# Projecting the gates' 48 columns with the linear attention's values, token groups of 304 and 256 columns

## The chip, the cores and the metric

One NeuronCore of a Trainium2 chip runs the whole kernel. The metric is the device time of one execution in microseconds (us). A profiled execution also has a span, from its first to its last instruction.

Engines are named as in the profile: PE is the matrix engine, PEld its weight loads, DVE, ACT and POOL the vector, scalar and GpSimd engines, and SP the engine that issues nearly all DMAs here, one after the other, in the order of its queue. Each engine works through its own queue in order.

## What is computed

Two layers of a diffusion backbone over 256 context tokens and 2048 latent tokens, 1024 wide. In each layer the modulated stream is multiplied by one combined input projection whose columns feed three branches: gated DeltaNet (a), neighbourhood attention (b) and gated linear attention (c, "GLA"). The branches are gated, concatenated, projected and normalised.

```python
(a_qkv_l, a_ab_l, a_z_l, b_q_l, b_k_l, b_v_l, b_z_l,
 c_q_l, c_k_l, c_v_l, c_r_l, c_z_l) = jnp.split(ml @ w_in[i], PROJ_SPLITS, axis=-1)
...
oa_c, oa_l = gdn_branch(a_qkv_c, a_ab_c, a_qkv_l, a_ab_l, conv_w[i], a_log[i], dt_bias[i])
ob_c, ob_l = na_branch(b_q_c, b_k_c, b_v_c, b_q_l, b_k_l, b_v_l, rpb[i], ctx_out)
oc_c, oc_l = gla_branch(c_q_c, c_k_c, c_v_c, c_r_c, c_q_l, c_k_l, c_v_l, c_r_l,
                        gla_w2[i], gla_b2[i])
```

The 48 columns of this document are `c_r` (32, from which GLA's decay gates come) and `a_ab` (16, from which the DeltaNet's gates come).

## The kernel before

The 2304 tokens are cut into six blocks of 384, each of three tiles of 128 tokens. The modulated stream of a block lies in DRAM (`M`), 1024 rows deep, as eight k-tiles. `Dense.run` multiplies it by a set of weight columns. Each float32 product is made of three fp32r products (high by high, high by low, low by high), so one output group is 8 k-tiles by 3, or 24 matmuls, all from the one line L197 in `dense_mm`. There are two kinds of groups:

- a channel group (`chan`) has the weights as the stationary operand and 384 tokens moving; its output is columns by tokens;
- a token group (`tok`) has one tile's 128 tokens as the stationary operand and up to 512 weight columns moving; its output is tokens by columns.

In each layer the runs come in this order, and in each run the blocks one after another, first the channel groups of a block and then the token groups of its three tiles:

1. the GLA run: channel groups of 48 (`O_CR` and `O_AB`), 128 (`O_CK`) and 128 (`O_CQ`) columns; token groups of 512 (`O_CV` and `O_CZ`). It also splits the stream into high and low parts (L186, L189) and writes them back to DRAM (`MS`). `gla.block` (lines from L405 on) follows each block in program order;
2. the attention run: four channel groups of 128 columns and token groups of 512 (`O_BV` and `O_BZ`);
3. runs for the DeltaNet's convolution (channel groups only) and, later, its output gate (`O_AZ`, token groups of 512).

In layer 1 the two context tiles have no output gates, so their token groups in the first two runs are 256 wide.

A k-tile sits in an SBUF buffer called `mm`; there are ten buffers (`MBUF`), eight for the block at work and two for the next one. A buffer of the old block comes free when the block's last token group has read it, and only then does SP load the next block's k-tile into it (L241 from `MS`, L244 from `M`). Outputs of groups go through PSUM tiles of a pool with two buffers (`psd`).

The callback of the 48-column group, `cb_r`, copies its output (L367), writes the 32 `c_r` rows to DRAM as `RC` (L368), and turns the `a_ab` part by three transposes on PE (L371) into `e.ab`. `gla.block` reads `RC` back as `rc` and makes the gates from it (matmuls `pg`, L425), after the rotation matmuls `pr` (L417). Then follow a chain on DVE and ACT (L427 to L465), products on POOL (`qkp`, L472), small matmuls (`pD` L476, `pA` and `pB` L494 and L501, 32 or 64 columns wide), and per 128 tokens the matmuls `pO`, `pk`, `pS` with their copies. `gla.reverse` (L552 on) ends the branch.

The program's order is made by a scheduler at build time: it places the instructions on the engines by program order, by readiness and by a priority that callbacks and splits are given. Matmuls of the two runs therefore stand between those of `gla.block`, and the attention run begins while `gla.block` is still at work.

## Time and profile before

| what | us |
|---|---|
| median of three runs | 3960.82 |
| the three runs | 3960.82, 3921.74, 3962.12 |
| the profiled execution | 3949.59 |
| its span | 3947.8 |
| PE busy in the span | 3618.4 (92%) |
| DVE busy | 2455.6 (62%) |
| ACT busy | 1687.4 (43%) |

Busy time counts a matmul from its start to its modelled end; matmuls that follow each other overlap, so the pace of a stream is read from the distance of the starts. The granted clock is given as a share of the full TensorE clock (1.00 is 2.4 GHz, 0.5 is 1.2 GHz; a stretch between them holds some of each). "x<-y" in a row names what is written and what is read; a bracket gives the idle time ahead of a row and who ended it.

### The profile page before, as it was taken

What the parts mean: (1) busy time and instruction counts of PE and PEld (TensorE: products, weight loads), DVE (VectorE), ACT (ScalarE), POOL (GpSimd) and SP (SyncE); (2) the same over time, 40 slices, a digit from 0 to 9 for tenths busy, and PEclk for the clock granted to TensorE, in tenths of its full rate; (3) what the DMA queues carried; (4) which work ended last, traced back from release to release, by engine and by line L of the source; (5) the groups of instructions that cost most, each with busy time, mean ns of one, the idle gap of its engine ahead of it and who ended that gap; (6) DMA issues with size and microseconds to landing.
All of it is one profiled execution on the core that took longest, in us unless ns stands there. A gap on an engine that the chain in (4) does not pass through costs nothing.

```text
span 3947.8 us, 76664 instructions
## 1 busy us (share of the span) xinstructions
PE 3618.4 (92%) x27262; PEld 3113.5 (79%) x27262; DVE 2455.6 (62%) x6983; ACT 1687.4 (43%) x4587; POOL 682.8 (17%) x1118
## 2 busy tenths in 40 slices
PE   6999999999989999998998999999999899989898
PEld 3787778769977888896776778777899688878787
DVE  4456463668966477446884655427788567653577
ACT  3533233435533455565544333333455235545531
POOL 0221111220102222220002211102102132222100
PEclk8988889999999799999997889899999888879899
DMA  9844325886687777766755444468665977685664
GB/s 294 284 133 141 124 84 167 264 264 198 208 271 227 223 210 208 211 204 213 238 178 172 141 129 137 131 202 246 202 213 193 324 207 213 194 215 171 218 204 125
DMA packets 756085, 787.55 MB, mean 199 GB/s; under 512 B 190206, under 2 KB 665206, under 8 KB 755702
## 3 DMA queue, kind: packets, MB, share of 16 engines
q1 hardware_dynamic: 755702, 782.64, 64.5%
q8 instruction: 216, 3.54, 0.4%
q14 instruction: 167, 1.37, 0.1%
HBM read 548.41 MB, written 234.03 MB: 198 GB/s over the span
## 4 chain that ended last, share of the span: by engine, by line
PE 60%; DMA 18%; DVE 13%; ACT 4%; SPq 2%; issue 2%; POOL 1%; DVEq 0%; ACTq 0%; POOLq 0%
PE p L197 29%; PE py L197 6%; DMA mm<-MS 3%; PE p L1258 3%; DMA gb<-GR 2%; DMA o<-OA 1%; PE pv L1022 1%; PE po L1042 1%; PE pd L1029 1%; DMA kk<-KK 1%; PE p L104 1%; PE pk L1011 1%; PE po L1044 1%; DVE acc L661 1%; PE pD L476 1%
## 5 line engine op out<-in xcount | busy, mean ns | idle before, releaser
L197 PE MATMUL p<-mm,wh 128*128 128x384 f32 (+1 forms) x3648 | 995.8, 352 | 51.9 <-DMA mm<-MS 32.4
L197 PEld LDWEIGHTS p<-mm,wh 128*128 128x128 f32 (+1 forms) x3648 | 661.3, 191 | 123.2 <-DMA mm<-MS 48.1
L197 PE MATMUL p<-mm,wl 128*128 128x384 f32 (+1 forms) x1824 | 630.0, 347 | 0.4 <-DVE wl L189 0.3
L197 PE MATMUL p<-wh,mm 128*128 128x512 f32 (+1 forms) x1696 | 566.5, 407 | 11.4 <-DMA mm<-MS 4.5
L197 PEld LDWEIGHTS p<-wh,mm 128*128 128x128 f32 x1696 | 329.4, 197 | 89.7 <-DMA mm<-MS 9.2
L661 DVE SCALAR_TENSOR_TENSOR acc<-pre,cw,acc 128x384 f32<-128x384 f32 (+1 forms) x576 | 358.3, 640 | 49.8 <-ACT acc L659 43.0
L197 PEld LDWEIGHTS p<-mm,wl 128*128 128x128 f32 (+1 forms) x1824 | 346.5, 190 | 16.1 <-issue 9.7
L197 PE MATMUL p<-wl,mm 128*128 128x512 f32 (+1 forms) x848 | 342.4, 404 | 1.2 <-DVE rst L395 1.0
L197 PEld LDWEIGHTS p<-wl,mm 128*128 128x128 f32 x848 | 167.3, 197 | 36.2 <-issue 2.2
L197 PE MATMUL py<-w,mh 128*128 128x512 f32 x544 | 178.8, 407 | 7.7 <-ACT mh L1380 5.0
L1004 POOL TENSOR_TENSOR kd<-kk,eD 128x256 f32<-128x256 f32 x144 | 89.3, 620 | 453.2 <-DMA kk<-KK 190.0
L1274 DVE SCALAR_TENSOR_TENSOR zt<-zt,p 128x256 f32<-128x256 f32 (+1 forms) x102 | 51.5, 507 | 178.9 <-ACT zt L1273 177.9
L1237 ACT ACTIVATE w<-w,mn 128x696 f32<-128x696 f32 (+2 forms) x136 | 112.8, 830 | 82.8 <-DVE mn L1234 80.0
L651 POOL COPY pre<-pre 128x4 f32<-128x4 f32 x120 | 81.0, 678 | 383.8 <-DVE acc L661 190.9
L925 DVE TENSOR_TENSOR tmp<-M 96x30 f32<-96x30 f32 (+4 forms) x360 | 126.6, 352 | 29.7 <-issue 21.9
L1015 DVE SCALAR_TENSOR_TENSOR R<-pk,neG,kk 128x128 f32<-128x128 f32 x272 | 81.4, 344 | 100.9 <-PE pk L1011 100.0
L865 DVE SCALAR_TENSOR_TENSOR gb<-gb,Gt,mats 128x128 f32<-128x128 f32 x288 | 86.4, 359 | 91.4 <-DMA gb<-GR 88.9
L1258 PE MATMUL p<-v,wl 120*128 120x64 f32 (+1 forms) x960 | 140.5, 285 | 0.0
L926 DVE TENSOR_TENSOR M<-M,tmp 96x30 f32<-96x30 f32 (+4 forms) x360 | 127.3, 354 | 6.3
L1258 PEld LDWEIGHTS p<-v,wl 120*128 120x128 f32 (+1 forms) x960 | 130.6, 204 | 0.7
L186 ACT CAST wh<-raw 128x512 fp32r<-128x512 f32 (+3 forms) x144 | 75.8, 555 | 123.6 <-DMA raw<-in_w_in 105.7
L189 POOL TENSOR_TENSOR mm<-mm 128x384 fp32r<-128x384 f32 x48 | 58.4, 1222 | 398.2 <-ACT mm L186 391.7
(307 smaller groups left out, 8136.1 us busy)
## 6 DMA issues: line engine op xcount, KB each, us to landing
mm<-MS SPq DMA_DIRECT2D x384, 384.0 KB
kk<-KK SPq DMA_DIRECT2D x144, 512.0 KB
MS<-mm SPq DMA_DIRECT2D x96, 384.0 KB
raw<-in_w_in SPq DMA_DIRECT2D x104, 256.0 KB
w<-in_w_mod SPq DMA_DIRECT2D x96, 256.0 KB
M<-m SPq DMA_DIRECT2D x36, 512.0 KB
mm<-M SPq DMA_DIRECT2D x96, 192.0 KB
KK<-kq SPq DMA_DIRECT2D x96, 192.0 KB
```

Source lines behind the costliest of these rows:

```text
L186: eng_hi.copy(hi, src)
L189: eng_lo.tensor_tensor(lo, src, hi.bitcast(F32), op=ALU.subtract)
L197: e.nc.tensor.matmul(p, x(k), y(k), start=n == 0, stop=n == 3 * KD - 1)
L651: nc.gpsimd.tensor_copy(pre[:, 0:4], pre[:, m:m + 4])
L661: nc.vector.scalar_tensor_tensor(acc[:, :n], pre[:, k:k + n], w(kind, k), acc[:, :n], op0=ALU.mult, op1=ALU.add)
L865: nc.vector.scalar_tensor_tensor(E[:, d, h], gb[:, d, h], self.G[:, d, c, h0 + h:h0 + h + 1], e.mats[:, 1 + d], op0=ALU.subtract, op1=ALU.min)
L925: nc.vector.tensor_tensor(tv, col, row, op=ALU.mult)
L926: nc.vector.tensor_tensor(o, o, tv, op=ALU.add)
L1004: nc.gpsimd.tensor_tensor(kd, kv[:, :, 0], self.eD[:, d, c, h0:h0 + 2].unsqueeze(2).to_broadcast([128, 2, 128]), op=ALU.mult)
L1015: nc.vector.scalar_tensor_tensor(R[:, h], pk[:, h], sc(self.neG, h), kv[:, h, 1], op0=ALU.mult, op1=ALU.add)
L1237: nc.scalar.activation(w[:, a, 0:256 + nk], w[:, a, 0:256 + nk], AF.Exp, bias=m[:, a:a + 1], scale=-1.0, accum_out=sm[:, a:a + 1])
L1258: nc.tensor.matmul(p[:, a], l, r, start=j == 0, stop=j == len(parts) - 1)
```

## The change

The 48-column channel group is gone. Its columns join the values' token group: `O_CV` (256) with `O_CR` (32), which lie side by side in the weights, and `O_AB` (16), 304 moving columns. The output gate's 256 columns (`O_CZ`) form a second token group. The attention run's 512 are cut into 256 (`O_BV`) and 256 (`O_BZ`) too, so that the weight tiles of both runs have like sizes. The new callback `cb_v` copies 304 columns, writes the values, copies 16 columns into `e.ab`, and turns the 32 `c_r` columns by one transpose per tile into a PSUM tile that fills up over the block's three tiles; the block's `RC` is written after the third. The separate weight pool `w0` falls away.

```diff
-    def cb_r(self, P, ps):
-        def f(p, b):
-            e, nc = self.e, self.e.nc
-            r = P.tile([48, BLK], F32, tag="r48", name="r48", bufs=1)
-            nc.scalar.copy(r, p)
-            nc.sync.dma_start(self.RC[b], r[0:32])
-            pt = ps.tile([128, TPB, 48], F32, tag="dn", name="pt")
-            for t in range(TPB):
-                nc.tensor.transpose(pt[:, t], r[:, t * 128:(t + 1) * 128], e.ident[0:48, 0:48])
-            nc.vector.tensor_copy(e.ab[:, b * TPB:(b + 1) * TPB], pt[:, :, 32:48])
-        return f
-
-    def cb_v(self, P):
-        def f(p, t):
-            v = P.tile([128, 256], F32, tag="bv", name="cv")
-            self.e.nc.scalar.copy(v, p[:, 0:256])
-            self.e.nc.sync.dma_start(self.V[t * 128:(t + 1) * 128], v)
+    def cb_v(self, P, ps):
+
+        def f(p, t):
+            e, nc = self.e, self.e.nc
+            v = P.tile([128, 304], F32, tag="cv", name="cv")
+            nc.scalar.copy(v, p[:, 0:304])
+            nc.sync.dma_start(self.V[t * 128:(t + 1) * 128], v[:, 0:256])
+            nc.vector.tensor_copy(e.ab[:, t], v[:, 288:304])
+            b, j = divmod(t, TPB)
+            if not j:
+                self.pr = ps.tile([32, BLK], F32, tag="dn", name="pr")
+            nc.tensor.transpose(self.pr[:, j * 128:j * 128 + 128], v[:, 256:288], e.ident)
+            if j == TPB - 1:
+                r = P.tile([32, BLK], F32, tag="r32", name="r32", bufs=1)
+                nc.scalar.copy(r, self.pr)
+                nc.sync.dma_start(self.RC[b], r)
         return f
...
-                        W0, WK, P, W = pool(g, "w0"), pool(g, "wk"), pool(g, "cb"), pool(g, "wc")
-                        zc, vc = z_cb(e, P, G2, 768, 256, 256), gla.cb_v(P)
-                        dn.run(W, [([(O_CR, 32), (O_AB, 16)], gla.cb_r(P, psh)), ([(O_CK, 128)], gla.cb_k(P)), ([(O_CQ, 128)], gla.cb_q(P))],
-                               [([(O_CV, 256), (O_CZ, 256)], cbc)], bufs=2, w0=W0, wk=WK, save=True, after=gla.block, width=lambda t: (512 if live(t) else 256,))
+                        WK, P, W = pool(g, "wk"), pool(g, "cb"), pool(g, "wc")
+                        zc = z_cb(e, P, G2, 768, 256, 0)
+                        dn.run(W, [([(O_CK, 128)], gla.cb_k(P)), ([(O_CQ, 128)], gla.cb_q(P))],
+                               [([(O_CV, 288), (O_AB, 16)], gla.cb_v(P, psh)), ([(O_CZ, 256)], zc)], bufs=2, wk=WK, save=True, after=gla.block,
+                               width=lambda t: (304, 256 if live(t) else 0))
                         gla.reverse()
-                        zb, vb = z_cb(e, P, G2, 512, 256, 256), na.cb_v(P)
+                        zb, vb = z_cb(e, P, G2, 512, 256, 0), na.cb_v(P)
                         dn.run(W, [([(o + 128 * hp, 128)], na.cb(P, k, hp)) for k, o in ((0, O_BQ), (1, O_BK)) for hp in range(2)],
-                               [([(O_BV, 512)], cbb)], bufs=2, wk=WK, width=lambda t: (512 if live(t) else 256,))
+                               [([(O_BV, 256)], vb), ([(O_BZ, 256)], zb)], bufs=2, wk=WK, width=lambda t: (256, 256 if live(t) else 0))
```

The scheduler then orders the program anew. Three places show it.

On PE, at the start of layer 1's GLA run, behind the last transposes of layer 0 (L153), before the change: the transposes of the 48-column group, the rotation `pr`, then the first context tile's values with the gate matmul `pg` eight matmuls later.

```order
L153 MATMUL p<-ident,x 128x128 x16
L371 MATMUL pt<-ident,r_23134 128x48 x3
L417 MATMUL pr<-qk_23286,mats 128x384 x2
L197 MATMUL p<-wh,mm 128x256 x2
L197 MATMUL p<-wl,mm 128x256
L197 MATMUL p<-wh,mm 128x256
L197 MATMUL p<-wl,mm 128x256
L197 MATMUL p<-wh,mm 128x256 x3
L425 MATMUL pg<-rc,w2p 128x384
```

In the changed program (line numbers are one lower) the same `pr` stands behind the same transposes, but `pg` stands behind three whole groups of 304, one of 256 and 38 channel matmuls of the next block. These are the rows around it.

```order
L197 MATMUL p<-mm,wh 128x384 x2
L197 MATMUL p<-mm,wl 128x384
L197 MATMUL p<-mm,wh 128x384 x2
L424 MATMUL pg<-rc,w2p 128x384 x2
L197 MATMUL p<-mm,wh 128x384
```

So the first block's gates moved behind all of that block's token groups.

On PE, at a change of block late in layer 1's attention run, before: the last token group's end and the next block's first channel group.

```order
L197 MATMUL p<-wl,mm 128x512
L197 MATMUL p<-wh,mm 128x512
L197 MATMUL p<-mm,wh 128x384 x2
L197 MATMUL p<-mm,wl 128x384
```

And in the changed program:

```order
L197 MATMUL p<-wl,mm 128x256
L197 MATMUL p<-wh,mm 128x256
L197 MATMUL p<-mm,wh 128x384 x2
L197 MATMUL p<-mm,wl 128x384
```

Nothing stands between the two groups in either; the group that reads the old k-tiles last is half as wide.

On SP, at such a change of block, before: the loads of the next block's k-tiles (`mm<-MS`) with the stores of the gates (`G`) and values (`Vb`) among them.

```order
L241 DMA mm<-MS_22919 128x2x384
L1275 DMA G_22867<-zt 128x256
L1108 DMA Vb<-bv 128x256
L241 DMA mm<-MS_22919 128x2x384 x5
L241 DMA mm<-MS_22920 128x2x384
```

And in the changed program:

```order
L241 DMA mm<-MS_23732 128x2x384
L1107 DMA Vb<-bv 128x256
L241 DMA mm<-MS_23732 128x2x384 x5
L1274 DMA G_23675<-zt 128x256
L241 DMA mm<-MS_23727 128x2x384 x2
```

One store left the place between the first load and the other five.

## Rows read from the trace of the kernel before

**Rows 1.** The page: busy us of each engine, share of the span, instructions.
```profile
PE 3618.4 (92%) x27262; PEld 3113.5 (79%) x27262; DVE 2455.6 (62%) x6983; ACT 1687.4 (43%) x4587; POOL 682.8 (17%) x1118
```

**Rows 2.** Busy time in stretches (us, instructions), granted clock, DMA share, GB/s.
```profile
core 0: us, PE busy (x) PEld busy (x) DVE busy (x) ACT busy (x) POOL busy (x), PEclk, DMA share, GB/s
75.00:345.00 270.00, 255.25 (x2083) 209.69 (x2083) 137.76 (x328) 120.88 (x274) 52.27 (x42) 0.90 0.65 211
345.00:706.00 361.00, 330.60 (x3230) 281.78 (x3229) 180.39 (x479) 115.00 (x319) 49.43 (x48) 0.85 0.40 128
2050.00:2380.00 330.00, 290.38 (x2747) 234.08 (x2745) 191.48 (x510) 125.55 (x254) 68.11 (x50) 0.82 0.50 160
2380.00:2680.00 300.00, 276.97 (x2227) 240.68 (x2226) 119.42 (x303) 90.61 (x275) 33.73 (x46) 0.91 0.50 158
```

**Rows 3.** Line L197, token matmuls by operands: ns min/median/max; first and last start.
```profile
L197 PE MATMUL p<-wh,mm x1696: 278/389/988, 94.6 to 3190.8; 128*128 128x512 f32 x181, 128*128 128x256 f32 x8
L197 PE MATMUL p<-wl,mm x848: 278/389/795, 94.8 to 3190.5; 128*128 128x512 f32 x164, 128*128 128x256 f32 x6
```

**Rows 4.** Timeline of PE: each pair lies three matmuls apart, widths 256, 512, 384.
```profile
2402.29 0.28 PE L197 MATMUL p<-wl,mm 128*128 128x256 f32 x1
2402.65 0.28 PE L197 MATMUL p<-wl,mm 128*128 128x256 f32 x1
...
2659.14 0.39 PE L197 MATMUL p<-wl,mm 128*128 128x512 f32 x1
2659.82 0.39 PE L197 MATMUL p<-wl,mm 128*128 128x512 f32 x1
...
2666.07 0.34 PE L197 MATMUL p<-mm,wl 128*128 128x384 f32 x1
2666.59 0.34 PE L197 MATMUL p<-mm,wl 128*128 128x384 f32 x1
```

**Rows 5.** The same at a change of block in layer 1's attention run.
```profile
2665.72 0.51 PE L197 MATMUL p<-mm,wh 128*128 128x384 f32 x2
...
2668.73 0.61 PE L197 MATMUL p<-mm,wh 128*128 128x384 f32 x2 [1.27 <-DMA mm<-MS]
...
2670.02 0.61 PE L197 MATMUL p<-mm,wh 128*128 128x384 f32 x2 [0.50 <-DMA mm<-MS]
```

**Rows 6.** Timeline of SP's queue at the same place.
```profile
2661.15 0.58 SPq L241 DMA_DIRECT2D mm<-MS  x1
...
2662.94 4.30 SPq L241 DMA_DIRECT2D mm<-MS  x6
```

**Rows 7.** Waits of PE for k-tiles, 2546 to 2685 us, then 2050 to 2680, then 75 to 706.
```profile
PE p L197 <- DMA mm<-MS: 8.6, 8, 2.1
...
PE p L197 <- DMA mm<-MS: 11.2, 11, 2.1
...
PE p L197 <- DMA mm<-MS: 3.4, 5, 1.5
```

**Rows 8.** Busy time and clock in two stretches of layers 0 and 1.
```profile
516.60:547.30 30.70, 29.74 (x332) 25.93 (x331) 11.90 (x41) 3.60 (x9) 3.83 (x4) 0.68 0.14 46
...
2600.00:2680.00 80.00, 73.02 (x355) 64.88 (x356) 20.37 (x36) 19.55 (x56) 4.79 (x14) 0.98 0.69 211
```

**Rows 9.** Timeline of PE: layer 1's first gate matmuls, and the chain's first wait.
```profile
2081.38 2.93 PE L417 MATMUL pr<-qk,mats 128*128 128x384 f32 x4 [1.65 <-ACT m L156]
...
2087.29 1.64 PE L425 MATMUL pg<-rc,w2p 32*128 32x384 f32 x2
...
2108.96 0.59 PE L476 MATMUL pD<-mats,qkp 128*128 128x4 f32 x2 [8.12 <-POOL qkp L472]
```

**Rows 10.** Callbacks, counted by tile: ns min/median/max.
```profile
L378 ACT COPY cv<-p x36: 350/372/423, 101.1 to 2377.3; 128x256 f32<-128x256 f32 x36
...
L371 PE MATMUL pt<-ident,r x18: 221/258/338, 2079.2 to 2330.5; 48*128 48x48 f32 x18
L367 ACT COPY r<-p x6: 454/472/473, 2053.2 to 2328.9; 48x384 f32<-48x384 f32 x6
```

More of the change, by code (lines that the diff above doesn't have):

```diff
@@ L1447, in layer @@
                     next(p1, None)
-        def cbc(p, t):
-            if live(t):
-                zc(p, t)
-            vc(p, t)
-        def cbb(p, t):
-            if live(t):
-                zb(p, t)
-            vb(p, t)
         with ExitStack() as gx:
```

## Prediction, before the changed kernel was run

> **What bounds the kernel now.** I read the page first. PE is busy for 92% of the span, and no other engine for more than 62% [rows 1]. An average hides stages, so I cut out the two stretches in which the edited runs lie: 75 to 706 us in layer 0 and 2050 to 2680 us in layer 1 [rows 2]. There PE is busy for 88 to 95% of the time, at a granted clock of 0.82 to 0.91, while DVE is busy for 40 to 58% and the DMA engines for 40 to 65%. So PE's own time, and what PE waits for, is the currency. The reader should see two things that the busy share does not tell. First, a matmul's duration is not its price: a 512-wide one takes 389 ns [rows 3], but in a stream it costs the distance of the starts. Three matmuls take 0.68 us at 512 columns, 0.52 at 384 and 0.36 at 256 [rows 4], so one costs 0.227, 0.173 and 0.120 us. Second, PE stands still where a block ends: after the last 512-wide group it runs three k-tiles of the next block and then waits 1.27 and 0.50 us for k-tiles still on their way [rows 5].
>
> **The columns.** The line through those three prices is 0.013 us a matmul and 0.417 ns a column; a 304-wide matmul, which the trace lacks, lies between two that it has, and the line gives 0.140 us. The token matmuls are 1696 + 848 = 2544 [rows 3]. The output-gate run of the DeltaNet has 34 groups of 24, 816 of them. The other 1728 are split evenly between the two edited runs: in each 816 of 512 columns (18 tiles in layer 0, 16 in layer 1) and 48 of 256 (layer 1's two context tiles). The 48-column group adds 24 matmuls for each of 12 blocks, 288, which cost the price of 384 moving columns, whatever their few outputs.
>
> - GLA run before: 816 x 0.227 + 48 x 0.120 + 288 x 0.173 = 185.2 + 5.8 + 49.8 = 240.8 us. After: 864 of 304 and 816 of 256, 121.0 + 97.9 = 218.9 us. That is 21.9 us less.
> - Attention run: each 512 becomes two of 256, 816 x (0.240 - 0.227) = 10.6 us more.
>
> Together 11.3 us less, at the full clock. Where the clock is granted at half, a column costs twice as much. Over the four stretches the mean is 0.87 [rows 2], so the gain lies between 11.3 and 11.3/0.87 = 13.0 us. I take **-12**.
>
> The Trainium skill (TensorE: Matmul & The Clock Gate, section Back-to-back issue gap) gives a lone warm matmul's gap as N/2.4 + 2.5 ns, and this trace disagrees: 256 columns come to 109 ns by it and 120 ns by the rows. With its smaller fixed cost the cut in the attention run would be nearly free (816 x 2.5 ns = 2 us) and the two runs would gain about 25 us by an estimate from that page.
>
> **The small work around it.** The transposes on PE stay 36 in number; each is a fraction of a microsecond [rows 10]. Three per block that stood together now stand apart, and each needs ACT's copy of its tile, but about 12 matmuls of the next group stand ahead of it. The value copy grows by 48 columns, from 0.37 us by at most the 0.10 us that separates it from a 384-wide copy [rows 10]; 36 of these and 24 more small DVE copies lie on engines that are half idle. The attention run's weights come in 32 loads instead of 16, each with a split on ACT and DVE, behind the four channel groups of the first block, 96 x 0.173 = 17 us of cover. All this I count at nothing; uncovered it would be some 10 us over both layers. Two gains of the same size stand against it and count nothing either: the value copy no longer shares a PSUM tile with the gate, and layer 1's values no longer wait for the gate's weights.
>
> **The lead of the loads.** This is the part that the column count does not show. A k-tile's buffer is free when the last token group of its block has read it. With 512 columns that group lasts 24 x 0.227 = 5.4 us, and its first k-tile is read through 21 matmuls, 4.8 us, before the end. The group that is last now has 256: the same point lies 21 x 0.120 = 2.5 us before the end. So SP can begin to load the next block 2.3 us later. The rows show that this lead is used up already: SP issues the first load at 2661.15, 4.6 us ahead of the next group, then (as the order shows) two stores, then six loads in 4.30 us, 0.72 us each [rows 6], and the loads issued at 2662.94 and 0.72 us later let PE go on only at 2668.73 and 2670.02 [rows 5], 5.8 and 6.4 us after their issue. Now one store fewer stands among them. First load 2.4 us ahead, one store 0.7, then five loads: the sixth load is issued at +1.9 us instead of at +0.1 (its two stores and four steps of 0.72 behind 2661.15). I take 2.0 us more standstill at each change of block where PE has nothing else.
>
> How many are those? There are 24 changes of block or run, 12 per layer. In before, PE's wait for k-tiles was 8.6 us in the 139 us in which only the attention run and what follows was left in layer 1, and 11.2 us over the whole of that layer's 630 us, against 3.4 us in layer 0 [rows 7]. So the wait gathers where GLA's small matmuls are over, and costs little where they give the loads time. By the order of the changed program, GLA's last matmul has 96 channel and 260 token matmuls of the attention run behind it in layer 0 and 192 and 403 in layer 1, which is 48 and 82 us at the prices above; a block of that run is 96 x 0.173 + 144 x 0.120 = 34 us. That makes two and three uncovered changes of block; in layer 1 one more stands among the few matmuls of the branch's reverse pass, six in all: **+12 us**. The bounds are 0 (the loads catch up because the DMA engines are half idle) and 24 x 2.3 = 55 us.
>
> **GLA's chain.** `RC` of a block is written after its third value group now, and in layer 1 the first `pg` moves behind 72 x 0.140 + 24 x 0.120 + 38 x 0.173 = 19.5 us of other matmuls, against 6 us from `pr` to `pg` before (2081.38 to 2087.29 [rows 9]). It is late by about 14 us. What is late next is `pD`, which already held PE for 8.12 us [rows 9] with values queued behind it. But the order fills this time with value groups, and behind the chain's end stand the 82 us of dense work. In layer 0 the order puts the first `pr` about 16 us of dense work earlier than before. I count nothing; the bounds are -8 (that standstill goes) and +14.
>
> **Sum.** 3949.6 - 12 + 12 = 3949.6, so **3950 us**. It is made against the profiled execution (3949.59), 11 us under the median of the runs shown (3960.82); those three differ by 40 us among themselves, so 1% is about what a measurement can tell from no change.
>
> **Rivals.**
>
> 1. *The columns' gain arrives whole.* The loads make up their lead, as with one store fewer and DMA engines at a share of 0.50 [rows 2] they might. For it: in layer 0 PE waited 3.4 us in all for k-tiles. Against it: the 5.8 to 6.4 us from issue to use. 3949.6 - 12 = 3938; with `pD`'s standstill gone as well, 3930.
> 2. *The lead is lost at every change of block.* Where GLA's work is mixed in, the last group is only 256 wide as well, and in the new order channel matmuls follow it at once at most of the 24 places. Then 3949.6 - 12 + 55 = 3993, slower by 1.1%. It decides when more than about 12/2.3 = 5 of the 24 places are uncovered, and passes 1% from 22 of them on. Against it: the 3.4 us of layer 0 [rows 7].
> 3. *The clock.* The small matmuls of `pA` and `pB` bring the granted clock to 0.68 in a stretch of 30.7 us, while the dense end of the stage has 0.98 [rows 8]. The changed order puts less dense work between the chain's steps (groups of about 3.4 us for 5.4), and more behind it. If the half-clock stretches shrink with the chain, the dense work that leaves them costs half: by the order 25 and 30 us of dense work move behind the chain in the two layers, and at a mean clock of 0.87 [rows 2] a quarter of it ran at half clock, a gain of up to 14 us and 3936. If PE waits for the chain instead, because 3 us do not cover its copies, each of 12 blocks has five such gaps; 0.5 us in each is 30 us and 3980. I hold the loss the likelier of the two.
>
> **How the numbers follow.** The forecast, gain and lost lead within some 15 us of each other (3935 to 3965), gets 0.45. Rival 1 and the gaining side of rival 3 get 0.27; one of them alone lies at 3930 to 3938, and the part more than 1% below (under 3910) needs both and the start of layer 1 as well. Rival 2 gets 0.15, and rival 3's loss, or late gates, 0.13. The range that leaves out no more than two in ten goes from 3915 to 3988: it holds all of the forecast, nearly all of the gains and the losses short of rival 2's end. The profiled time is one of several that differ by as much, so some of each side falls beyond 1%: for faster by over 1% I give 0.17, within 1% 0.63, slower by over 1% 0.20.
>
> **What would show it.** Pace: 304-wide matmuls start 0.140 us apart at full clock and 256-wide ones 0.120. Columns: line L197 has 864 matmuls of 304 columns and none with 48 outputs. Lead: at a change of block in the late attention run, PE waits about 4 us for `mm<-MS` in place of 1.8, and the wait over 2050 to 2680 grows from 11.2 us towards 19. Chain: layer 1's first `pg` stands some 14 us later after its `pr`, and GLA's last matmul earlier, with about 82 us of dense work behind it. I am wrong if the sum of PE's waits for k-tiles stays where it was (then rival 1), if it grows at changes of block among GLA's matmuls too (rival 2), or if waits of `pO`, `pS` and `pA` for DVE and ACT, or the granted clock of the two stretches, move by more than 10 us or 0.03 (rival 3).

## The result: about 1% slower

The changed kernel took 3989.86 us (median of four runs, 3965.39 to 4006.17) against 3956.81 us for the kernel before: a ratio of 1.0125, 95% interval 1.0081 to 1.0169; the two medians by themselves make 1.0084. Timed again in a later series, twelve runs of its own against 35 of before, the ratio was 1.0093 (1.0062 to 1.0123). The forecast was 3950 us with a range of 3915 to 3988. The sign of the columns was right and the sum was wrong by some 40 us. Ratios here and below leave out the few slow executions of a series, so they need not be the quotient of two medians.

The page and the waits of PE over the whole span, after; the first line answers to [rows 1]:

```profile
PE 3637.8 (91%) x28606; PEld 3209.6 (80%) x28606; DVE 2470.9 (62%) x7031; ACT 1688.1 (42%) x4611; POOL 666.2 (17%) x1118
...
L197 PE MATMUL p<-mm,wh 128*128 128x384 f32 x3456 | 948.9, 354 | 80.8 <-DMA mm<-MS 47.4
L197 PE MATMUL p<-wh,mm 128*128 128x256 f32 (+2 forms) x2784 | 681.5, 333 | 38.6 <-DVE zt L1273 16.1
```

```profile
PE p L197 <- DMA mm<-MS: 52.4, 45, 6.7
...
PE p L197 <- DVE zt L1273: 20.5, 16, 3.4
...
PE p L197 <- ACT wh L186: 9.3, 4, 6.9
PE p L197 <- ACT bv L1106: 8.8, 5, 2.9
```

The same waits in before:

```profile
PE p L197 <- DMA mm<-MS: 36.9, 36, 3.5
...
PE p L197 <- ACT wh L186: 4.3, 3, 2.4
...
PE p L197 <- DVE zt L1274: 2.2, 2, 1.5
```

(The columns of the last two fences: engine, tile and line that wait, what they wait for, us in total, times, longest. Lines behind the edit are one lower than before.) Two things are to be seen. Channel groups wait longer for k-tiles, as forecast. And a wait that was next to nothing before, 2.2 us, is now 20.5 us, the second longest of L197: token groups wait for `zt` and `bv`, that is for the ACT and DVE operations that copy a finished group out of its PSUM bank.

The columns themselves cost what was worked out. The timeline of PE has three 304-wide matmuls in 0.42 us and three 256-wide ones in 0.36:

```profile
2324.75 0.28 PE L197 MATMUL p<-wl,mm 128*128 128x256 f32 x1
2324.87 0.40 PE L197 MATMUL p<-wh,mm 128*128 128x256 f32 x2
2325.11 0.28 PE L197 MATMUL p<-wl,mm 128*128 128x256 f32 x1
...
2329.23 0.31 PE L197 MATMUL p<-wl,mm 128*128 128x304 f32 x1
2329.37 0.44 PE L197 MATMUL p<-wh,mm 128*128 128x304 f32 x2
2329.65 0.30 PE L197 MATMUL p<-wl,mm 128*128 128x304 f32 x1
```

**A ledger.** The time of PE can be split without the busy share. The starts of all matmuls are taken in two stretches: layer 0 from 60 us to the last output matmul of its DeltaNet, and layer 1 from the last matmul of layer 0's output projection to the same point. Each L197 matmul is charged 0.013 us and 0.417 ns a column, the prices of the prediction. Where the granted clock was half when it ran, what its start-to-start distance has above that, up to its columns once more, is put down to the clock. What is left up to the next start is standstill behind an L197 matmul. The last part is all time from the start of another matmul to the next start, its waits included. In us, both layers:

| kernel | L197 at full-clock prices | L197 at half clock | L197 standstill | other matmuls | total |
|---|---|---|---|---|---|
| before | 1513.6 | 61.7 | 175.7 | 1653.5 | 3404.5 |
| before, second profile | 1513.6 | 66.9 | 173.0 | 1650.7 | 3404.2 |
| after | 1502.2 | 95.8 | 212.2 | 1641.5 | 3451.7 |
| after, second profile | 1502.2 | 86.4 | 210.3 | 1629.0 | 3427.9 |

The first column counts matmuls and takes the prices as given: 11.4 us less, as the prediction had it. The prices themselves hold too: the matmuls at full clock that came within 15% of their price, some 7000 before and 7900 after, took in all 11 and 6 us more than they were charged. The means of two profiles give a loss of 36 us: 11 us less for columns, 37 us more standstill of L197, 27 us more for L197 matmuls at half clock, and 17 us less behind the others.

**The clock of the dense matmuls.** The mean granted clock doesn't show that part: it is 0.910 before and 0.912 and 0.918 after, and in the two stretches of the next table the time at half clock did not grow (347 and 349 us before, 350 and 317 after). What changed is which matmuls lay in it. In the ledger's stretches 407 and 422 matmuls of L197 started at half clock before, 765 and 674 after. In the stretches of the next table the half-clock time fell into 23 and 28 pieces before, and into 39 in both profiles after. A 256-wide matmul then cost 0.213 us in place of 0.120, as the rows below from 172.85 us on show at a granted clock of 0.50.

What the standstill is called shows in PE's waits, added up by what they wait for over the two stretches in which the edited runs lie (685 us from 60 us on, 690 us from 30 us ahead of layer 1's start). "Banks" are waits of L197 for `zt`, `bv`, `cv`, `cqk` and `nqk`; "GLA" are all waits of the branch's own small matmuls.

| kernel | banks | k-tiles | weights | GLA | others | sum |
|---|---|---|---|---|---|---|
| before | 8.0 | 18.0 | 4.9 | 59.7 | 31.4 | 122.0 |
| before, second profile | 6.8 | 16.9 | 5.0 | 56.9 | 28.8 | 114.4 |
| after | 40.7 | 28.7 | 11.4 | 39.5 | 24.9 | 145.2 |
| after, second profile | 38.2 | 31.6 | 11.6 | 39.5 | 25.1 | 146.0 |

The two profiles of one kernel agree within 3 us in each column but the sum of before (7.6 us), so differences of 5 us in a cause can be read, though the total time of single runs differs by 20. The sum rises by 27 us; with 27 us for the dense matmuls at half clock and 11 us less for columns that makes 43 us, against the ledger's 36.

**How a bank is late.** The place is layer 0, where GLA's first chain runs. The fences are the timelines of PE, of ACT and of DVE in the changed kernel.

```profile
168.25 0.30 PE L197 MATMUL p<-wh,mm 128*128 128x304 f32 x1
168.39 0.72 PE L475 MATMUL pD<-mats,qkp 128*128 128x4 f32 x6
172.47 0.58 PE L197 MATMUL p<-wh,mm 128*128 128x256 f32 x1 [3.36 <-DVE zt L1273]
172.85 0.41 PE L197 MATMUL p<-wl,mm 128*128 128x256 f32 x1
173.06 0.63 PE L197 MATMUL p<-wh,mm 128*128 128x256 f32 x2
173.49 0.41 PE L197 MATMUL p<-wl,mm 128*128 128x256 f32 x1
```

```profile
166.68 0.37 ACT L1272 ACTIVATE zt<-p 128x256 f32<-128x256 f32 x1
```

```profile
168.79 0.34 DVE L444 TENSOR_TENSOR a<-B 128x192 f32<-128x192 f32 x1
169.06 0.35 DVE L443 TENSOR_TENSOR a<-B 128x192 f32<-128x192 f32 x1
...
172.01 0.41 DVE L1273 SCALAR_TENSOR_TENSOR zt<-zt,p 128x256 f32<-128x256 f32 x1
```

The last matmul of a gate's group started at 164.81 us, ACT's tanh on it began at 166.68, and the DVE operation that reads the bank for the last time ran only at 172.01, behind a row of GLA's decay operations (`a<-B`, 0.34 us each and back to back). PE filled the other bank with a 304-wide group, ran six small matmuls from 168.39 us on, and then had no bank: 3.36 us of standstill. The group that had waited then ran at half clock. Of the 18 and 17 waits for banks over 1 us in the two profiles, 7 and 6 had dense matmuls at half clock within 4 us behind them. DVE is busy for about half of this stretch on the mean (354 of 685 us), which says nothing of such a burst. From the tanh's start to the end of the DVE operation a 256-wide gate usually takes 0.84 us, in before and after alike. It took more than 2.9 us, the length of a 256-wide group, for 9 of 68 gates before and for 16 and 18 of 68 in the two profiles after. Before, PE had 5.4 us of the next 512-wide group as cover, and where the delay was longer (six of the nine, up to 8.1 us) GLA's small matmuls, channel groups or another wait lay in the same time: none of the nine shows a wait for `zt`.

**The k-tiles.** PE's waits for them, 75 to 738 us and 2075 to 2725 us of after, which answer to the 3.4 and the 11.2 us of [rows 7] (in layer 0 the window of [rows 7] ends at 706 us, just ahead of the end of the attention run, where before waits 2.18 us):

```profile
PE p L197 <- DMA mm<-MS: 16.0, 12, 6.6
...
PE p L197 <- DMA mm<-MS: 12.7, 10, 6.7
```

Over the whole span they are 52.4 us, and 53.4 in the second profile, against 36.9 and 41.2 before. They don't lie where I put them. The changes of block inside the late attention run did not grow in layer 1 and grew by some 5 us in layer 0; one new long wait stands where that run ends, in each layer. That end is also the place of [rows 5, 6]: behind 2665.72 us of before no token matmul of the attention run follows, so what I read there as a change of block inside the run is the step to the conv stage, 1.27 and 0.50 us of waiting. Timelines of PE and SP of after at the same place:

```profile
2708.76 0.34 PE L197 MATMUL p<-mm,wl 128*128 128x384 f32 x1
2715.76 1.01 PE L197 MATMUL p<-mm,wh 128*128 128x384 f32 x2 [6.66 <-DMA mm<-MS]
```

```profile
2699.05 0.58 SPq L241 DMA_DIRECT2D mm<-MS  x1
2700.04 0.33 SPq L1107 DMA_DIRECT2D Vb<-bv  x1
2700.47 1.94 SPq L241 DMA_DIRECT2D mm<-MS  x3
2702.45 0.59 SPq L712 DMA_DIRECT2D al<-in_a_log  x1
...
2708.63 1.38 SPq L102 DMA_DIRECT2D w<-in_w_mod  x3
2710.05 0.29 SPq L98 DMA_DIRECT2D b<-in_b_mod  x1
2710.45 1.88 SPq L241 DMA_DIRECT2D mm<-MS  x3
```

Before, six loads stood together on SP and the next stage's small loads came behind them:

```profile
2662.94 4.30 SPq L241 DMA_DIRECT2D mm<-MS  x6
2667.29 0.72 SPq L713 DMA_DIRECT2D al<-in_a_log  x1
```

Now those loads (gate constants, masks, taps, modulation weights) stand in the middle, 8 us of issue, and three k-tiles wait behind them: PE waits 6.66 us where it waited 1.77. The new order of SP's queue, which the scheduler made, cost more than the 2.0 us that I had priced for a place.

**Layer 1's start.** The first gate matmuls came later than forecast, `pg` 36 us behind `pr` where it was 6 [rows 9], but the chain's wait at `pD` became shorter, 3.27 us for 8.12:

```profile
2106.59 1.01 PE L416 MATMUL pr<-qk,mats 128*128 128x384 f32 x1 [2.14 <-ACT m L156]
...
2142.76 0.91 PE L424 MATMUL pg<-rc,w2p 32*128 32x384 f32 x2
...
2158.38 0.59 PE L475 MATMUL pD<-mats,qkp 128*128 128x4 f32 x2 [3.27 <-POOL qkp L471]
```

And the layer's first group now waits 6.9 us for its weights, in place of 2.4: the 24 matmuls of the 48-column group, 4.2 us, had run while those weights came in. In both kernels the group behind starts 7.0 and 7.3 us after the last matmul of layer 0 (2048.58 to 2055.58 us before, 2073.22 to 2080.51 after).

### The profile page after: what moved, and what is told of

Its sections match the earlier page's. It is cut to its first block, busy times and chain, and to the rows that moved or that the text cites. A ratio compares the mean times of both kernels' runs of the same rounds, so it can differ in the third digit from the quotient of the medians.

```text
span 3994.6 us, 79487 instructions
## 1 busy us (share of the span) xinstructions
PE 3637.8 (91%) x28606; PEld 3209.6 (80%) x28606; DVE 2470.9 (62%) x7031; ACT 1688.1 (42%) x4611; POOL 666.2 (17%) x1118
## 4 chain that ended last, share of the span: by engine, by line
PE 60%; DMA 21%; DVE 9%; ACT 4%; SPq 3%; issue 2%; POOL 0%; DVEq 0%; ACTq 0%; POOLq 0%
PE p L197 29%; PE py L197 6%; DMA mm<-MS 4%; PE p L1257 3%; DMA raw<-in_w_in 2%; DMA gb<-GR 2%; PE p L104 2%; PE pv L1021 1%; DMA o<-OA 1%; PE pA L493 1%; PE pd L1028 1%; PE po L1041 1%; DMA x<-in_x 1%; DMA mm<-M 1%; PE pz L967 1%
## 5 line engine op out<-in xcount | busy, mean ns | idle before, releaser
L197 PE MATMUL p<-mm,wh 128*128 128x384 f32 x3456 | 948.9, 354 | 80.8 <-DMA mm<-MS 47.4
L197 PEld LDWEIGHTS p<-mm,wh 128*128 128x128 f32 x3456 | 640.5, 196 | 139.1 <-DMA mm<-MS 69.2
L197 PE MATMUL p<-wh,mm 128*128 128x256 f32 (+2 forms) x2784 | 681.5, 333 | 38.6 <-DVE zt L1273 16.1
L197 PE MATMUL p<-mm,wl 128*128 128x384 f32 x1728 | 597.4, 348 | 0.0
L197 PEld LDWEIGHTS p<-wh,mm 128*128 128x128 f32 x2784 | 499.3, 205 | 81.0 <-DVE zt L1273 20.1
L197 PE MATMUL p<-wl,mm 128*128 128x256 f32 (+2 forms) x1392 | 455.6, 327 | 2.1 <-DVE wl L189 2.1
L660 DVE SCALAR_TENSOR_TENSOR acc<-pre,cw,acc 128x384 f32<-128x384 f32 (+1 forms) x576 | 353.3, 633 | 53.4 <-ACT acc L658 49.8
L197 PEld LDWEIGHTS p<-mm,wl 128*128 128x128 f32 x1728 | 336.3, 195 | 9.8 <-issue 8.9
L197 PEld LDWEIGHTS p<-wl,mm 128*128 128x128 f32 x1392 | 285.9, 205 | 16.1 <-DVE wl L189 3.1
L197 PE MATMUL py<-w,mh 128*128 128x512 f32 x544 | 178.4, 406 | 9.4 <-ACT mh L1379 5.3
L189 DVE TENSOR_TENSOR wl<-raw,wh 128x512 fp32r<-128x512 f32 (+3 forms) x168 | 90.8, 555 | 79.3 <-ACT wh L186 78.2
L197 PEld LDWEIGHTS py<-w,mh 128*128 128x128 f32 x544 | 101.9, 193 | 33.2 <-ACT mh L1379 7.5
```

Of the source, the lines that this page charges most:

```text
L189: eng_lo.tensor_tensor(lo, src, hi.bitcast(F32), op=ALU.subtract)
L197: e.nc.tensor.matmul(p, x(k), y(k), start=n == 0, stop=n == 3 * KD - 1)
L660: nc.vector.scalar_tensor_tensor(acc[:, :n], pre[:, k:k + n], w(kind, k), acc[:, :n], op0=ALU.mult, op1=ALU.add)
```

## The experiments

The theories: **banks** (groups of 3 us leave two PSUM banks too little time to be emptied), **k-tiles** (the lead that the prediction priced at 12 us), **columns** (the cut of the attention run, 10.6 us), and **order** (the changed order of GLA's work by itself). Ratios are against the kernel before in the same series, with 95% intervals.

| kernel | median us | ratio | interval |
|---|---|---|---|
| after again | 3973.38 | 1.0093 | 1.0062 to 1.0123 |
| before again | 3952.34 | 1.0026 | 0.9985 to 1.0068 |
| a_attn512 | 3951.59 | 1.0046 | 1.0013 to 1.0079 |
| b_cut | 3990.83 | 1.0131 | 1.0092 to 1.0171 |
| a_zbank | 3940.92 | 0.9997 | 0.9971 to 1.0024 |
| a_mbuf12 | 3967.53 | 1.0064 | 1.0033 to 1.0095 |
| b_bank3 | 3922.07 | 0.9952 | 0.9925 to 0.9978 |
| a_bank3 | 3902.12 | 0.9909 | 0.9876 to 0.9943 |
| a_attn512_zbank | 3922.86 | 0.9968 | 0.9939 to 0.9997 |
| a_attn512_bank3 | 3898.89 | 0.9905 | 0.9874 to 0.9936 |
| a_hold | 4018.29 | 1.0216 | 1.0183 to 1.0250 |
| b_hold | 3950.74 | 1.0037 | 1.0010 to 1.0064 |
| a_early | 3990.39 | 1.0116 | 1.0072 to 1.0160 |
| a_zbank_early | 3936.27 | 0.9978 | 0.9951 to 1.0005 |
| a_bank3_early | 3926.08 | 0.9952 | 0.9916 to 0.9988 |

The kernel before against itself came to 1.0026, so a difference of 0.3% between two rows is not to be read.

### The two runs apart

```diff
# a_attn512: the changed kernel, attention run at 512 again
-[([(O_BV, 256)], vb), ([(O_BZ, 256)], zb)], ... width=lambda t: (256, 256 if live(t) else 0))
+[([(O_BV, 512)], cbb)], ... width=lambda t: (512 if live(t) else 256,))
# b_cut: the kernel before, its attention run's 512 columns issued as two groups of 256
+tg = [((wh[:, :, o:o + 256], wl[:, :, o:o + 256], 256), c) for o, c in zip((0, 256), cut)]
```

> The changed kernel with the attention run's value and output gate columns in one group of 512 again; the GLA run keeps its groups of 304 and 256. Columns alone give back 10.6 us of the 3990. If the standstills came with the cut in the attention run (k-tiles that are 15 us later, values and gates not yet out of PSUM, 25 us), they go as well: 3940 to 3955, and the waits of L197 for the value copy fall to about 0. If they come from the GLA run and from its changed order, 3979, and only the columns are seen.

> The kernel before with nothing changed but that each 512-wide token group of the attention run is issued as two of 256 (weights still loaded as 512). By columns 3957 + 10.6 = 3968. If the narrower groups bring the standstills (lead of the loads +15, PSUM not yet empty +20 to +25), 3990 to 4005, with new waits for the value copy and the gate of some 10 us a layer. If the standstills belong to the GLA run, 3968 and k-tile waits as before (32 us on the page).

The cut alone costs 1.31% in the kernel before, as much as the whole change; a_attn512 still costs 0.46% although its columns are 21.9 us less. In the waits of the two stretches b_cut's k-tiles rise from 17 to 38.9 us and its banks only to 13.2; a_attn512 has k-tiles at 13.1 and banks at 25.3. L197 at half clock takes 68.2 us in b_cut and 82.3 in a_attn512, against 61.7 and 66.9 before. So the two parts of the change have different faults: the narrow last group of the attention run goes with the late k-tiles, the two narrow groups between GLA's operations with the late banks and with more dense work at half clock. Whole span, b_cut and a_attn512:

```profile
PE p L197 <- DMA mm<-MS: 62.2, 53, 7.1
```

```profile
PE p L197 <- DMA mm<-MS: 30.9, 32, 3.4
...
PE p L197 <- DVE zt L1280: 12.5, 8, 3.8
```

The prices don't add up to the whole (1.31% and 0.46% against 0.93 to 1.25%), and b_cut has 30 us more of standstill and time behind other matmuls, where its named waits in the two stretches are 8 us more; that remainder has no name. No run gave b_cut a third bank, so how its 1.31% arises stays open.

### A third bank

In both edited runs the pool `psh` gives the small transposes' tile two PSUM buffers, which follow each other block by block; the kernels below leave it one. a_zbank gives it to the output gate's groups; the bank3 kernels put it into rotation for all groups of these runs, in the changed kernel and in the one before.

```diff
# a_zbank
-p = ps.tile([128, wd], F32, tag="dn", name="p")
+p = (zp if zp and i else ps).tile([128, wd], F32, tag="dn", name="p")
# a_bank3, b_bank3
-e, ps = self.e, self.ps
+e, rot = self.e, [self.ps, self.ps, zp or self.ps]
...
+rot.append(rot.pop(0))
+p = rot[0].tile([128, wd], F32, tag="dn", name="p")
```

> The changed kernel with the output gate's token groups in a PSUM bank of their own, so that channel and value groups share two and the gates have a third (the bank that held a second, unused copy of the transposes' tile). If the evacuation of groups of 3 us over two banks is a cause, the page's waits of L197 for the gate (zt) and the value copy (bv) fall from some 29 us to under 10 and the time to 3965 to 3975. If only the lead of the loads or the changed order counts, 3990 and the time goes into other waits.

> The kernel before with a third PSUM bank in rotation for the channel and token groups of the two edited runs; nothing else. Groups of 512 last 5.4 us, and the profile of before has 2 us of waits for the gate in all, so if the bank heals what the change broke, it is worth nothing here: ratio 0.998 to 1.002. If a third bank is a gain for any kernel of this form, 0.990 to 0.995, and the gain seen with the gate's own bank says nothing on the change.

> The changed kernel with a third PSUM bank in rotation, exactly as in the kernel before with a third bank (0.9952). If the change's loss is mainly the banks, the two now differ by the columns (-11 us) and the k-tiles that come late at the end of the attention run (+10 us): 0.993 to 0.998. If other standstills are the larger part, 1.000 or more.

With two banks the change loses 0.93 to 1.25%; with three the changed kernel is at 0.9909 and the one before at 0.9952, so the change gains about 0.4%, with intervals that overlap a little. The third bank takes some 1.9% from the changed kernel and 0.5% from the one before, a difference far beyond the intervals: the loss hangs on having two banks. My expectations missed on three counts: the third bank is not worth nothing in the kernel before, a_zbank's 3940.92 us lies below its 3965 to 3975 though its waits for banks, 15.4 us, are not under 10, and a_bank3 lies below its 0.993. Ledger and waits:

| kernel | L197 at half clock | L197 standstill | other matmuls | total | banks | k-tiles |
|---|---|---|---|---|---|---|
| after, mean of two | 91.1 | 211.3 | 1635.3 | 3439.8 | 39.5 | 30.2 |
| a_zbank | 53.5 | 188.2 | 1644.8 | 3388.8 | 15.4 | 29.9 |
| b_bank3 | 64.9 | 143.3 | 1662.9 | 3384.7 | 6.1 | 4.3 |
| a_bank3 | 53.7 | 177.2 | 1598.7 | 3331.7 | 6.5 | 25.7 |
| a_bank3_early | 51.9 | 162.2 | 1645.2 | 3361.5 | 9.4 | 12.9 |

The bank gives back more than the waits that carry its name. In a_zbank 24 us of waits for banks go, and 38 us of dense matmuls at half clock with them: 414 L197 matmuls start there, as many as before the change, and its half-clock time in the two stretches is again in 23 pieces. With all groups in rotation the same 37 us go (387 matmuls in a_bank3). The profiled execution of a_bank3 took 3878.49 us, 24 us less than the median of its six, so its total and its 1598.7 us are not to be read to the us; a_bank3_early, further below, has the same half-clock part. What brings the dense matmuls out of the half-clock pieces is not separated by these runs: a third bank also changes the order in which the program's instructions are laid out, and PE that gets past a late bank reaches GLA's next matmul sooner. That a gate is late on DVE is unchanged: 13 of 68 gates in a_bank3 still take more than 2.9 us, but PE no longer stands. In layer 0 L197 has no wait over 1.2 us before 602 us, where the changed kernel with two banks has six. The waits of PE in a_bank3:

```profile
PE p L197 <- DMA mm<-MS: 46.2, 34, 6.9
...
PE p L197 <- ACT wh L186: 8.1, 3, 6.5
...
PE p L197 <- DVE nqk L1082: 3.9, 2, 2.7
...
PE p L197 <- DVE zt L1275: 2.4, 5, 0.7
```

b_bank3 has a loss of its own. In layer 0 dense work was done so early that GLA's reverse pass was left alone at the end; the trace has ACT and SP in that pass (`sq<-o`, `OC`, `QD`) while PE waits for the conv stage's first weights:

```profile
704.11 1.01 PE L197 MATMUL p<-mm,wh 128*128 128x384 f32 x2 [25.33 <-ACT wh L186]
```

So part of the 0.4% between the two kernels with three banks may be this place and not the columns; without it they might be equal. The 0.5% of the kernel before are not explained by its banks' waits, which were 7 us and are 6; its waits for k-tiles fell from 17 to 4.3 us.

The Trainium skill (Perfetto Trace Analysis, Optimizing Tensor Performance, Matmuls) says that independent groups should rotate through PSUM banks so that the evacuation of one overlaps the next group's matmuls. This case's trace agrees, and the number of banks matters in it: with two, waits for banks were 7 us in the two stretches with groups of 5.4 us and 39 us with groups of 3 us, beside a DVE with bursts of 5 us.

### Banks held longer

```diff
+for _ in range(2 if n == 256 else 0):
+    nc.scalar.copy(th[:, :n], z)
 nc.scalar.activation(th[:, :n], z, AF.Tanh, scale=0.5)
```

> The changed kernel with each 256-wide gate copied twice more by ACT out of PSUM ahead of its tanh (into the tile that the tanh then overwrites), which holds the group's bank some 0.7 us longer and adds about 50 us of work to an ACT that is 42% busy. If the banks of the 3-us groups come free too late for PE, each gate now costs more: the waits of L197 for zt grow from 20 us to 40 or more, and the time by 15 to 40 us, to a ratio of 1.014 to 1.020 against before. If the banks are not what is late, 1.009 to 1.012 as without the copies.

> The kernel before with the same two extra copies of each gate. Its groups last 5.4 us at 512 columns, so the longer hold has room: ratio 1.000 to 1.003. If it costs here what it costs in the changed kernel (1.004 or more), the copies' price is ACT's time and not the narrower groups.

The time moved the way the bank theory says, and by more: +0.9 to +1.2% in the changed kernel, just beyond the range, and +0.4% in the one before, between the two readings that I gave for it. The waits did not. `zt` fell from 20.5 us to 15.8 over the span, all banks' waits in the two stretches from 39 us to 24.8, and GLA's own waits in the two stretches rose from 39.5 us to 67.9; in before the banks' waits rose from 7 to 29 us. a_hold:

```profile
PE pD L475 <- POOL qkp L471: 19.5, 10, 4.7
...
PE p L197 <- DVE zt L1275: 15.8, 12, 2.4
```

The copies lie on ACT among the exponentials of GLA's chain, which they may delay; that is not shown apart. The pair shows that the changed kernel has less room on the engines that empty the banks; it doesn't show that the banks are it.

### The k-tiles

```diff
# a_mbuf12: 12 k-tile buffers in the two edited runs
+dn.buffers(g, 12)
# *_early: the conv stage's first k-tile loads written ahead of that stage's other loads
+nxt = dn.block(0, False)
```

> The changed kernel with 12 k-tile buffers for 10 during the two edited runs (room from sharing buffers that are used at other times). Next block's third and fourth k-tile no longer wait for this block's last group, and four loads instead of six stand in the burst at a change of block. If the lead of the loads is a cause, L197's wait for k-tiles falls from 47 us to 25 or less and the time to 3965 to 3975. If not, the wait stays over 40 or the time at 3990.

> The changed kernel (two PSUM banks) with nothing edited but that the conv stage's first k-tile loads are written ahead of the loads that prepare that stage. This undoes the one long wait for k-tiles that is new, 6.7 us at the end of the attention run in each layer against 2.2 and 1.3 us before. If the k-tiles are the smaller part of the loss, as the banks now suggest, 8 to 10 us go: a ratio of 1.007 to 1.009 instead of 1.010. If they are the larger part, 1.003 or less.

> The kernel with the gate's own bank, and the loads of the conv stage's first block written ahead of the loads that prepare that stage (gate constants, masks, taps, modulation weights). If the 6.7 us for k-tiles at the end of the attention run come from those loads standing ahead of the k-tiles on SP, they fall to about 2 us in both layers and the time by 8 to 10 us against the kernel with the bank alone (ratio 0.997). If the narrow last group alone makes them, they stay at 5 us or more and the time stays.

> The changed kernel with three PSUM banks in rotation and the conv stage's first k-tile loads written first. The profile with three banks still has 6.1 and 7.0 us of waiting for k-tiles where the attention run ends. If that price is on the path, 3902 - 9 = 3893, a ratio of 0.988 to 0.990; if the wait only goes elsewhere, 0.991.

The early loads did what they should to the wait. In a_early the conv stage's first group waits 3.6 us in layer 0 and 3.0 in layer 1 (6.6 and 6.7 without the edit), and the k-tiles of the two stretches fall from about 30 us to 22.3; in a_bank3_early from 25.7 to 12.9. The time did not follow: 1.0116 where the changed kernel had 1.0093 and 1.0125, and 0.9952 against 0.9909 with three banks, slower if anything; both expectations missed. Part of the wait went elsewhere in a_early: over the whole span its k-tiles are 48.3 us against 52.4 and 53.4, with 5.8 us of waiting later in the conv stage. a_zbank_early, 0.9978 against 0.9997, is inside the noise. So the late k-tiles are real and as long in sum as I priced them, but shortening the longest of them gave no measurable time back. a_early:

```profile
743.00 0.61 PE L197 MATMUL p<-mm,wh 128*128 128x384 f32 x2 [3.62 <-DMA mm<-MS]
```

a_mbuf12 is 0.3 to 0.6% faster than the changed kernel, but not by a clean edit: handing over from the 12 buffers to the 10 of the next stage cost a standstill of 12 us in each layer. Its waits for k-tiles did not fall as expected but rose, from 30 to 40.9 us in the two stretches, while its banks' waits fell from 40 us to 20.5.

```profile
707.04 0.98 PE L197 MATMUL p<-mm,wh 128*128 128x384 f32 x2 [12.21 <-DMA mm<-MS]
```

### Versions that beat both

> The changed kernel with the attention run back at 512 columns and, in the GLA run, the output gate's groups in a PSUM bank of their own. The columns are then 22 us fewer than before and none is paid for a cut in the attention run. If the standstills are those of two banks and of the narrow last group, both are gone but for the GLA run's last groups: 3942 - 22 = 3920, a ratio of 0.994 to 0.997. If the GLA run's changed order has a cost of its own, 1.000 or more.

> The attention run at 512 columns, the GLA run at 304 and 256, and the third bank in rotation. The columns are 22 us below before, the k-tiles come early again and no group waits for its bank: 0.9952 less 0.0055 is 0.990, if dense work that is done sooner does not leave the branch's reverse pass alone at the end of the stage, as it did for 25.7 us in layer 0 of the kernel before with the third bank; with that, 0.995 to 0.998.

The GLA run at 304 and 256 columns, the attention run at 512, and three banks: 0.9905 of before. It does not beat a_bank3 (0.9909), although it saves 10.6 us of columns more; in layer 0 it has a standstill of 19 us for the conv stage's weights, as b_bank3 has one of 25. With the third bank given to GLA's gates alone, a_attn512_zbank, it is 0.9968, and 1.0046 without the bank: in the GLA run by itself the bank is worth 0.8%.

### The two kernels again

> The changed kernel once more, unedited, for a second profile and a tighter ratio. If its loss is what the first runs show, the ratio is again 1.010 to 1.015; the wait of 6.7 us for k-tiles where the attention run ends and the wait of 7.0 us for the first weights of layer 1 are there again, since the order of the program makes them, and the single waits for zt and bv differ in place but not in sum (25 to 30 us).

> The kernel before once more, for a second profile: which of the standstills that are compared stay put between two executions. The stretch from layer 0's start to the end of its DeltaNet, 1726 us in the first profile against 1751 and 1750 in the two of the changed kernel, should repeat within 5 us if the 25 us there are the change's; layer 1's, in which the changed kernel's own two profiles differ by 24 us, may not.

The long waits came back in the same places: 6.4 and 6.5 us at the ends of the attention runs and 6.4 us at layer 1's start. From 60 us to the end of layer 0's DeltaNet the two profiles of the changed kernel take 1750.9 and 1750.3 us, those of before 1725.7 and 1731.2. In layer 1 the changed kernel's differ by 24 us (1701.4 and 1677.9) and those of before by 6 (1679.1 and 1673.1), so of single profiles only layer 0 repeats to about 5 us.

## Why the prediction was wrong

- **Columns: right.** -11.3 us at full clock, -11.4 by the ledger's count, at prices that held within 11 us over both layers. The 304-wide matmul, which the trace of before lacked, cost the 0.140 us that lies on the line through [rows 4].
- **The small work around it: the step that failed.** It was counted at nothing, with ACT and DVE "half idle" as the cover. The work itself is small indeed. What was not asked is how long a bank may be held. With two banks the next group is the cover that is always there for emptying one, and the change cut it from 5.4 to 2.9 or 3.4 us. Banks' waits went from 7 to 39 us, and a third bank took back the whole loss (0.9997 with it for the gate alone, 0.9909 in rotation). The row that should have warned is in the trace of before: 9 of 68 gates took longer than 2.9 us from tanh to the last read.
- **The clock: left out of the sum, and the wrong way.** The sum has only the columns' share at half clock, 0.7 us. Dense matmuls at half clock cost 64 us extra before, 91 after and 54 with a third bank. Rival 3 had seen that dense work may change its clock, but priced only the gain, as work that leaves the half-clock stretches; here more of it came to lie in them. Its sign, a mean clock that moves by 0.03, could not show this. Why it came is not shown.
- **The lead of the loads: the size was right, the place and the worth were not.** I forecast +12 us of k-tile waits; in the two stretches they rose by 12.7 us (17.5 to 30.2, means of two profiles). That the sums agree is luck: of the six places that I counted, those in layer 1 did not grow (11.2 us became 12.7 there, of which 6.7 are the run's end, not the forecast 19). The long new ones stand at the ends of the attention runs, through the order of SP's queue, and shortening those gave no time back. [rows 5, 6], from which I read the lead, already lie at such an end and not at a change of block.
- **Weights at layer 1's start: not priced.** The removed 48-column group was itself the cover for the next group's weights; its 4.2 us came back as 4.5 us of waiting (6.9 for 2.4).
- **GLA's chain: direction right, size off.** `pg` came 30 us later, not 14, and that cost nothing I can see; GLA's own waits fell from 58 to 39.5 us. I had counted that at nothing, within bounds of -8 to +14.
- **Rivals.** Rival 2's sign and time (3993) came true through another mechanism than its own: k-tile waits among GLA's matmuls are a small part. Rival 3 had PE wait for the chain's copies and priced 30 us; PE waited for the copies of its own groups instead. The mean clock did not move: the page's is 0.912 after and 0.910 before. The two edited stretches in after, which answer to [rows 2]:

```profile
345.00:738.00 393.00, 355.88 (x3593) 326.50 (x3592) 184.34 (x490) 119.22 (x338) 49.15 (x58) 0.87 0.46 142
2075.00:2430.00 355.00, 303.22 (x3113) 269.41 (x3114) 205.26 (x557) 136.17 (x285) 68.13 (x52) 0.84 0.49 157
2430.00:2725.00 295.00, 268.57 (x2499) 249.03 (x2498) 120.28 (x312) 85.97 (x264) 31.61 (x44) 0.92 0.49 156
```

**What stays open.** That the loss hangs on two banks is shown by the third. How its gain comes about is shown only in part: 24 to 33 us are waits that carry the banks' names, 37 us are dense matmuls that no longer run at half clock, and no run tells whether the bank itself or the order that comes with it moved those. The cut of the attention run alone, b_cut, costs 44 us in the ledger's stretches: 11 us of columns, 4 us at half clock, 8 us of named waits, and the other half has no name. Whether the change is worth anything with three banks in both kernels is open too, since b_bank3's 25 us belong to one place.

## What to carry to other kernels

Before a matmul group is cut or narrowed, compare its length with the time for which its PSUM bank is held, at the worst burst of the engines that empty it and not at their mean load; if the group is the shorter one, add a bank first, and try that bank on the old kernel too. A group that is removed may have been the cover of the next one's weights, and a buffer that comes free later can move a whole queue. A wait in a trace is not yet a price: here 13 us of waiting for k-tiles could be taken away without any gain, while 24 us of waiting for banks went together with 38 us that no wait named. And a mean clock can stand still while the dense work moves under the low one: count the dense matmuls that start there.

## What was not expected of the hardware

Two executions of one program agreed within 0.5 us over 3404 us of PE's work (before), but by luck: layer 0 took 5.5 us more and layer 1 6.0 us less. Two others (after) differed by 24 us, all of it in layer 1, at mean granted clocks of 0.912 and 0.918; there the time behind matmuls other than L197 was 796.5 and 773.7 us. Single profiles can therefore be compared by named waits, which repeated within 3 us, sooner than by their spans.

With a third bank the clock under the dense matmuls changed as much as the waits did: 765 and 674 of them started at half clock with two banks, 414 and 387 with three, at almost the same half-clock time (350 and 317 us against 320 and 312).
